# A hybrid decoder step on one core: the sample group's experts all run beside the second block, the low parts of weights are read back by two blocks, the background is spread anew, and attention's score products alternate row halves

## The chip, the cores and the metric

The kernel runs on one core of a Trainium2 chip. The metric is the device time of one execution in microseconds (us). A profiled execution gives the trace from which all rows below come; its time is shown beside its span.

## What is computed

One decoder layer for a prompt of 1024 tokens and a sample group of 8 sequences with 8 tokens each, width 1024. The two groups share all weights. Shortened:

```python
xn = rmsnorm(x, norm1_g)
xr, gr, q, k, v, ga, gb = split(xn @ w_in)              # 1024 x 5632
h  = rg_lru(causal_conv(xr)) ; lru_out = h * gelu(gr)
attn = window_attend(rmsnorm(q), rmsnorm(k), v, sinks)  # window 128, 16 heads on 4 key heads
merged = sigmoid(ga) * (lru_out @ w_branch_lru) + sigmoid(gb) * (attn @ w_branch_attn)
hres = x + merged @ w_out
xt = rmsnorm(hres, norm2_g)
# retrieval: 8 heads, 2 x 128 keys, the 16 best of each, then the best 16 pairs of each head
idx, g = top_pairs(xt @ w_query, sub_keys)              # 128 experts of 16384 for each token
act = gelu(einsum('cd,ced->ce', xt, expert_u[idx])) * g
y = hres + einsum('ce,ced->cd', act, expert_v[idx])
```

The outputs are y for both groups and the new convolution, recurrence and key/value caches.

## The kernel before

**Blocks.** The 1088 tokens go through the layer in three blocks: 256 prompt tokens with the 64 sample tokens, then 384, then 384 prompt tokens. `trunk` does a block in this order: queries, keys and values and the attention (`attention`), the branch of attention (loop of `w_branch_attn`, 8 column chunks), the recurrence (`lru`), the branch of the recurrence (8 chunks), the output product with `w_out` (4 column groups), the second norm (`norm_T`), and the retrieval (`retrieve`). The first norm of the next block (`norm1(bi + 1)`) stands just ahead of `w_out`, and two of the next block's projections (`EARLY`) ahead of the retrieval. After the three blocks, `dense` runs all 16384 experts for 640 prompt tokens, and beside it the last block's 384 tokens fetch their experts row by row.

**Products in two parts.** Each weight chunk of 128 x 1024 numbers is split in a high part (a cast on ScalarE, ACT) and a low part (a subtraction on VectorE, DVE, `split`, L164), and each product is three matmuls (L183 to L185). `wsplit` keeps the low parts of the first block's 84 chunks in HBM (`lo_d`); the third block reads them back (L209) instead of subtracting. High and low parts have three buffers each (`NW = 3`).

**Background.** What a block's retrieval leaves is done beside the next block by a generator, `behind(b)`: first `choose` (17 steps for each token tile: the best pairs of each head), then `build_g`, which turns the prompt tokens' chosen experts into a dense table of gates for `dense` (8 steps of four tokens make a chunk of 32 tokens: 64 steps for block 0, 96 for block 1). A step of `build_g` is two compares on DVE (L940, L941), four scalings on ACT (L943), four products on TensorE (PE, L923; the trace shows each as two instructions) into a PSUM buffer, and a copy by ACT into `sg` (L924). `bg(k)` takes k steps; `PG1` and `PG2` say how many at each place of the second and third block: index 0 after each chunk of the attention branch, 1 after each of six turns of the recurrence, 2 after each chunk of its branch, 3 after each column group of `w_out`, 4 after each tile of the second norm, 5 after each of 16 groups of the retrieval, 6 after each of five parts of q, k and v, 7 after each of 12 score groups. What is left runs at the block's end.

**The sample group's experts** are background too, since their 64 tokens were chosen in block 0. Two rows of partitions share a token, so 64 gathers of 128 rows (512 KB each, issued by GpSimd, POOL, L963) bring the rows of `expert_u`, and DVE multiplies and sums each (`early_u`, L965); 64 more bring `expert_v` (`early_v`, L978, L983). Each uses three row buffers in turn. In the kernel before, `early_u` runs beside the second block and `early_v` beside the third.

**One tile that three things share.** `at` (one buffer) holds a block's keys and values during attention, then the row buffers of `early_u` or `early_v` (tile `et`), then `sg` of `build_g`. PSUM tiles of the tag `tr` (three buffers) serve the transposes of the norms (L268), the products of `build_g` (L923) and the scores of the retrieval (L767). Tiles of one tag are handed out in the order of the program.

**Order.** Each engine carries out its instructions in a fixed order that a scheduler makes ahead of time; SyncE (SP) issues the loads in such an order as well.

Of the kernel before, what the change touches and what calls it, by code (L numbers as in the profile page):

```python
# [14 lines left out]
ALU = mybir.AluOpType  # L15
# [4 lines left out]
P = 128  # L20
# [8 lines left out]
HD = 64  # L29
# [9 lines left out]
SLOPES = [float(np.float32(2.0) ** np.float32(-8.0 * (h + 1) / NH)) for h in range(NH)]  # L39
# [19 lines left out]
NR = 3  # L59
GBL = 1  # L60
PG0 = (0, 0, 0, 0, 0, 0, 0, 0)
PG1 = (5, 5, 4, 5, 2, 2, 0, 0)
PG2 = (6, 6, 5, 1, 2, 4, 2, 2)
LATE = 3
VJ = 1
EARLY = (4, 0)
# [4 lines left out]
def f32(ap):  # L71
    return ap.bitcast(F32)


class Kern:
# [125 lines left out]
    def wsplit(self, key, hi, lo, raw):  # L201

        nc = self.nc
        m = self.chunk.setdefault(key, len(self.chunk))
        use = self.uses[key] = self.uses.get(key, 0) + 1
        kept = self.lo_d[m].rearrange("p (k c) -> p k c", c=raw.shape[2])
        if use == 3:
            nc.scalar.copy(hi, raw)
            nc.sync.dma_start(f32(lo), kept)  # L209
            return  # L210
        self.split(hi, lo, raw)
        if use == 1:
            nc.gpsimd.dma_start(kept, f32(lo))

    def load_c(self, src, c0):

# [79 lines left out]
    def trunk(self, bi, x, raw, bg):  # L296
# [4 lines left out]
        xh, xl = x  # L301
        self.pg = (PG0, PG1, PG2)[bi]
        self.at_free = False
# [98 lines left out]
    def attention(self, bi, xh, xl, ah, al, raw, bg):  # L402
        tc, nc, i, o, sp = self.tc, self.nc, self.i, self.o, self.sp
# [9 lines left out]
        kT = at[:, 2304:2304 + NKV * KC].rearrange("p (k c) -> p k c", k=NKV)  # L413
# [35 lines left out]
        def scores(t, j, qT):  # L449

            c0 = t * P
            first = bi == 0 and t == 0
            b0 = P if first else 0
            S = 2 * P - b0
            sb = sp.tile([P, 4, 256], F32, tag="sb", name="sb", bufs=6)
            for par in range(2):

                pss = self.mm().rearrange("p (g s) -> p g s", s=256)
                pr = slice(par * HD, par * HD + HD)
                for g2 in range(2):  # L460
                    nc.tensor.matmul(pss[:, g2, 0:S], qT[pr, 2 * j + g2, :], kT[pr, j, c0 + b0:c0 + 2 * P], start=True, stop=True)
                for g2 in range(2):
                    g = 2 * g2 + par
                    nc.vector.scalar_tensor_tensor(sb[:, g, 0:S], self.distP[:, b0:], -SLOPES[4 * j + g],
                                                   pss[:, g2, 0:S], op0=ALU.mult, op1=ALU.add)
            sm = sp.tile([P, 4, 4], F32, tag="sm", name="sm", bufs=3)
            m4, z4, e4, nm = (sm[:, x, :] for x in range(4))
            sk = self.snk[:, 4 * j:4 * j + 4]
            nc.vector.tensor_reduce(m4, sb[:, :, 0:S], axis=AX.X, op=ALU.max)
            nc.vector.tensor_tensor(m4, m4, sk, op=ALU.max)  # L470
            nc.vector.tensor_scalar(nm, m4, -1.0, None, op0=ALU.mult)
            nc.vector.tensor_tensor(e4, sk, m4, op=ALU.subtract)
            for g in range(4):
                nc.scalar.activation(sb[:, g, 0:S], sb[:, g, 0:S], AF.Exp, bias=nm[:, g:g + 1], accum_out=z4[:, g:g + 1])
            nc.scalar.activation(e4, e4, AF.Exp)
            nc.vector.tensor_tensor(z4, z4, e4, op=ALU.add)
            nc.vector.reciprocal(z4, z4)
            nc.vector.tensor_tensor(sb[:, :, 0:S], sb[:, :, 0:S], z4.unsqueeze(2).to_broadcast([P, 4, S]), op=ALU.mult)
            return sb
# [28 lines left out]
        for t in range(NT):  # L508
            qT = sp.tile([P, KD, P], F32, tag="sb", name="qT", bufs=6)
            for h in range(2):  # L510
                pt = self.tr()
                for k in range(4):
                    c = (h * 4 + k) * P
                    nc.tensor.transpose(pt[:, k, :], qn[:, t, c:c + P], self.ident)
                nc.scalar.activation(qT[:, 4 * h:4 * h + 4, :], pt, AF.Copy, scale=self.qg[:, 0:1])
            for j in range(NKV):
                late.append((t, j, scores(t, j, qT)))
                bg(self.pg[7])
                if t == 0 and j == (1 if smp else VJ):
                    self.qkv(bi, 5, xh, xl, lambda t, r: vd[0:r, t])  # L520
                if len(late) > (1 if smp else LATE) and (t or j >= VJ):
                    weigh(*late.pop(0))
# [469 lines left out]

    def behind(self, b):

        early, left = None, True
        ch = self.choose(b)
        while left or early is not False:
            if early is None and self.es is not None and self.at_free:
                early = self.early_v() if b else self.early_u()
            if left:  # L1000
                left = next(ch, None) is not None
            if early and next(early, None) is None:
                early = False
            yield True
        for _ in self.build_g(b):
            yield True
# [203 lines left out]
```

## Time and profile before

| what | value |
|---|---|
| median of 3 runs | 3771.19 us (3761.95 to 3776.55) |
| the profiled execution | 3777.02 us, span of its instructions 3775.2 us |
| PE busy / DVE / ACT / POOL | 90% / 77% / 39% / 41% of the span |
| moved by DMA | 968.36 MB, mean 257 GB/s |
| TensorE clock granted, mean | 0.945 of full speed |

The profiled execution is 5.8 us above the median of the runs. In the page, "busy" is the time in which an engine carries out at least one instruction; matmuls are pipelined, so that two of 0.34 us each can start 0.17 us apart. The stretch from the second block to the start of `dense` lies between 489 and 1820 us, `dense` between 1820 and 3775 us.

### The profile page before, as it was taken

The numbers are of one execution on the slowest core, as the hardware profiler recorded it, in microseconds if no ns is written. First come the engines' busy times: TensorE is split into PE (matmuls) and PEld (weight loads), VectorE is DVE, ScalarE is ACT, GpSimd is POOL, SyncE is SP. The second block draws the span as 40 slices with busy tenths as digits, with TensorE's granted clock in tenths as the row PEclk, the third lists the DMA queues.
The fourth block names the chain that finished last, engine by engine and source line by source line (L and its number), as shares of the span: only waits on it lengthen the run. The fifth ranks groups of instructions, "written<-read, shape, count | busy, mean of one in ns | idle before, by whom it ended". The sixth has DMA issues, their size and how long they took to land. (4 is left out here: it accounts for less than half of the span.)

```text
span 3775.2 us, 59354 instructions
## 1 busy us (share of the span) xinstructions
PE 3401.7 (90%) x21891; PEld 3244.8 (86%) x21891; DVE 2889.4 (77%) x6727; ACT 1453.8 (39%) x2969; POOL 1539.4 (41%) x1240
## 2 busy tenths in 40 slices
PE   6898999868898998769779999999999999999996
PEld 6798978758795887668679999999999999999995
DVE  6567797998689975546999777777777776778777
ACT  4555345445854473676222222222222222222220
POOL 0011100340000222000367676767667776777774
PEclk8899999879998999889789999999999999999998
DMA  7388833776552899645478898989989899899897
GB/s 229 108 260 283 264 97 96 242 231 220 183 187 69 272 320 344 238 159 199 162 259 285 314 311 289 312 298 321 311 298 319 307 316 312 310 320 318 310 310 276
DMA packets 539235, 968.36 MB, mean 257 GB/s; under 512 B 38108, under 2 KB 356508, under 8 KB 535840
## 3 DMA queue, kind: packets, MB, share of 16 engines
q0 software_dynamic: 141120, 513.86, 38.1%
q1 hardware_dynamic: 397824, 450.70, 37.5%
q8 instruction: 172, 2.82, 0.3%
q14 instruction: 119, 0.97, 0.1%
HBM read 860.10 MB, written 105.99 MB: 256 GB/s over the span
## 5 line engine op out<-in xcount | busy, mean ns | idle before, releaser
L183 PE MATMUL ou<-ah,vh 128*128 128x256 f32 (+1 forms) x2048 | 637.0, 315 | 58.7 <-DVE dac L1078 30.5
L183 PE MATMUL sc<-dx,uh 128*128 128x256 f32 (+1 forms) x2048 | 636.6, 311 | 11.0 <-DMA gt<-g_d 8.7
L185 PE MATMUL sc<-dx,ul 128*128 128x256 f32 (+1 forms) x2048 | 635.4, 311 | 1.3 <-POOL ul L164 1.3
L184 PE MATMUL sc<-dx,uh 128*128 128x256 f32 (+1 forms) x2048 | 636.2, 311 | 0.0
L184 PE MATMUL ou<-al,vh 128*128 128x256 f32 (+1 forms) x2048 | 632.0, 311 | 3.5 <-DVE al L164 3.2
L185 PE MATMUL ou<-ah,vl 128*128 128x256 f32 (+1 forms) x2048 | 630.3, 310 | 2.5 <-POOL vl L164 2.5
L903 DVE SCALAR_TENSOR_TENSOR acc<-row,hv,acc 128x1024 f32<-128x1024 f32 x384 | 493.6, 1285 | 147.7 <-DMA row<-in_expert_v,iA 145.5
L891 DVE SCALAR_TENSOR_TENSOR row<-row,xt 128x1024 f32<-128x1024 f32 x384 | 464.9, 1216 | 133.6 <-DMA row<-in_expert_u,iA 126.3
L889 POOL DMA_INDIRECT row<-in_expert_u,iA x384 | 366.4, 954 | 279.5 <-DVE row L891 193.2
L901 POOL DMA_INDIRECT row<-in_expert_v,iA x384 | 360.8, 940 | 273.3 <-DVE acc L903 189.9
L183 PEld LDWEIGHTS ou<-ah,vh 128*128 128x128 f32 x2048 | 387.5, 190 | 77.9 <-DVE dac L1078 40.3
L164 POOL TENSOR_TENSOR ul<-un,uh 128x1024 fp32r<-128x1024 f32 x128 | 308.0, 2406 | 330.2 <-DMA gt<-g_d 303.4
L183 PEld LDWEIGHTS sc<-dx,uh 128*128 128x128 f32 x2048 | 392.0, 191 | 12.2 <-ACT uh L163 9.0
L184 PEld LDWEIGHTS ou<-al,vh 128*128 128x128 f32 x2048 | 389.3, 190 | 6.0 <-DVE al L164 5.4
L185 PEld LDWEIGHTS sc<-dx,ul 128*128 128x128 f32 x2048 | 390.9, 191 | 2.1 <-POOL ul L164 2.1
L184 PEld LDWEIGHTS sc<-dx,uh 128*128 128x128 f32 x2048 | 391.9, 191 | 0.0
L185 PEld LDWEIGHTS ou<-ah,vl 128*128 128x128 f32 x2048 | 388.4, 190 | 2.7 <-POOL vl L164 2.7
L1078 DVE TENSOR_TENSOR dac<-dac,ou 128x384 f32<-128x384 f32 (+1 forms) x672 | 314.9, 482 | 46.0 <-PE ou L185 44.9
L163 ACT CAST uh<-un 128x1024 fp32r<-128x1024 f32 x128 | 134.5, 1051 | 496.3 <-PE sc L184 366.7
L164 POOL TENSOR_TENSOR vl<-vn,vh 128x1024 fp32r<-128x1024 f32 x128 | 308.9, 2419 | 16.0 <-ACT vh L163 14.3
L978 POOL DMA_INDIRECT et<-in_expert_v,est x64 | 71.6, 1119 | 585.0 <-DVE oi L940 389.6
L183 PE MATMUL mm<-xh,whi 128*128 128x384 f32 (+1 forms) x768 | 260.1, 339 | 20.1 <-ACT Ti L687 16.8
(294 smaller groups left out, 7655.8 us busy)
## 6 DMA issues: line engine op xcount, KB each, us to landing
wraw<-in_w_in SPq DMA_DIRECT2D x132, 512.0 KB
un<-in_expert_uT SPq DMA_DIRECT2D x128, 512.0 KB
vn<-in_expert_v SPq DMA_DIRECT2D x128, 512.0 KB
lo_d<-wlo POOLq DMA_DIRECT2D x84, 512.0 KB, 5.9
wlo<-lo_d SPq DMA_DIRECT2D x84, 512.0 KB
g_d<-sg SPq DMA_DIRECT2D x20, 2048.0 KB
wraw<-in_peer_w_query SPq DMA_DIRECT2D x48, 512.0 KB
gt<-g_d SPq DMA_DIRECT2D x32, 768.0 KB
```

Source lines behind the costliest of these rows:

```text
L163: nc.scalar.copy(hi, src)
L164: return (lo_eng or nc.vector).tensor_tensor(lo, src, f32(hi), op=ALU.subtract)
L183: nc.tensor.matmul(ps, lh, rh, start=first and j == 0, stop=False)
L184: nc.tensor.matmul(ps, lh, rl, start=False, stop=False)
L185: nc.tensor.matmul(ps, ll, rh, start=False, stop=last and j == n - 1)
L889: nc.gpsimd.indirect_dma_start(out=row, out_offset=None, in_=i["expert_u"], in_offset=bass.IndirectOffsetOnAxis(ap=ia[:, s:s + 1], axis=0))
L891: nc.vector.scalar_tensor_tensor(row, row, 1.0, xt, op0=ALU.mult, op1=ALU.mult, accum_out=hv[:, s:s + 1])
L901: nc.gpsimd.indirect_dma_start(out=row, out_offset=None, in_=i["expert_v"], in_offset=bass.IndirectOffsetOnAxis(ap=ia[:, s:s + 1], axis=0))
L903: nc.vector.scalar_tensor_tensor(acc, row, hv[:, s:s + 1], acc, op0=ALU.mult, op1=ALU.add)
L978: nc.gpsimd.indirect_dma_start(out=row(s), out_offset=None, in_=self.i["expert_v"], in_offset=bass.IndirectOffsetOnAxis(ap=self.es[:, 0, s ...
L1078: nc.vector.tensor_tensor(ac[k // 4][:, k % 4, a:b], ac[k // 4][:, k % 4, a:b], ps[:, 0:b - a], op=ALU.add)
```

## The change

Four things change. `behind` runs `early_u` and then `early_v` beside the second block, two steps of them with each step of `choose` until both are done, and none beside the third. `wsplit` reads the low parts back in the second block too. The tables `PG1` and `PG2` have new numbers; `PG2` takes 22 steps in the third block's attention (34 before). In `scores`, the four products of a group are written one after the other with the upper and the lower row half in turn, into two PSUM tiles taken at once.

```diff
-PG1 = (5, 5, 4, 5, 2, 2, 0, 0)
-PG2 = (6, 6, 5, 1, 2, 4, 2, 2)
+PG1 = (6, 5, 4, 5, 2, 2, 0, 0)
+PG2 = (5, 5, 4, 3, 2, 2, 2, 1)
@@ wsplit
-        if use == 3:
+        if use > 1:
             nc.scalar.copy(hi, raw)
             nc.sync.dma_start(f32(lo), kept)
             return
         self.split(hi, lo, raw)
-        if use == 1:
-            nc.gpsimd.dma_start(kept, f32(lo))
+        nc.gpsimd.dma_start(kept, f32(lo))
@@ attention, scores
-            for par in range(2):
-
-                pss = self.mm().rearrange("p (g s) -> p g s", s=256)
-                pr = slice(par * HD, par * HD + HD)
-                for g2 in range(2):
-                    nc.tensor.matmul(pss[:, g2, 0:S], qT[pr, 2 * j + g2, :], kT[pr, j, c0 + b0:c0 + 2 * P], start=True, stop=True)
...
+            pss = [self.mm().rearrange("p (g s) -> p g s", s=256) for _ in range(2)]
+            for g in range(4):
+                pr = slice(g % 2 * HD, g % 2 * HD + HD)
+                nc.tensor.matmul(pss[g % 2][:, g // 2, 0:S], qT[pr, 2 * j + g // 2, :], kT[pr, j, c0 + b0:c0 + 2 * P], start=True, stop=True)
...
@@ behind
-        early, left = None, True
+        early, left = False if b else None, True
         ch = self.choose(b)
         while left or early is not False:
             if early is None and self.es is not None and self.at_free:
-                early = self.early_v() if b else self.early_u()
+                early = itertools.chain(self.early_u(), self.early_v())
             if left:
                 left = next(ch, None) is not None
-            if early and next(early, None) is None:
-                early = False
+            for _ in range(2):
+                if early and next(early, None) is None:
+                    early = False
             yield True
```

The fixed order of the changed kernel, in two places. Its line numbers after L212 are one lower than before, after L455 three lower (L920 is L923 of before, L267 is L268, L962 is L965, L980 is L983).

The first place is the end of `w_out` in the second block. On DVE, changed kernel (`hr` takes the output product, `et` are the rows of the sample group's experts, `eh` their weights, `oij` and `oi` the compares of `build_g`):

```order
L356 TENSOR_TENSOR hr<-hr,mm 128x256
L962 SCALAR_TENSOR_TENSOR et,eh<-et 128x1024
L356 TENSOR_TENSOR hr<-hr,mm 128x256 x2
L962 SCALAR_TENSOR_TENSOR et,eh<-et 128x1024 x4
L965 TENSOR_TENSOR eh<-eh,est 128x64
L978 TENSOR_SCALAR et<-et,eh 128x1024
L980 SCALAR_TENSOR_TENSOR et<-et,eh 128x1024 x63
L985 TENSOR_TENSOR et<-et 64x1024
L986 TENSOR_TENSOR et<-et 64x1024
L938 TENSOR_TENSOR oij<-iof,sT 128x512 x2
```

Behind the last `hr` stand the last four rows of `early_u` and all 64 of `early_v`, with nothing between them, and then `build_g`. On PE, the same place before (`gh`, `gl` are the operands of `w_out`, `xn` the rows that a norm transposes):

```order
L185 MATMUL mm<-whi,gl 128x256
L923 MATMUL tr<-oij 128x128 x64
L268 MATMUL tr<-ident,xn 128x128 x4
L183 MATMUL mm<-whi,xh 128x256
L184 MATMUL mm<-wlo,xh 128x256
```

and in the changed kernel:

```order
L185 MATMUL mm<-whi,gl 128x256
L920 MATMUL tr<-oij 128x128 x92
L267 MATMUL tr<-ident,xn 128x128 x4
L183 MATMUL mm<-whi,xh 128x256
L184 MATMUL mm<-wlo,xh 128x256
```

16 steps of `build_g` (64 products) stood between `w_out` and the next norm's transposes, now 23 do (92), and none of these that needs `sg` can be copied out before `early_v` has left `at`.

The second place is the end of `w_out` in the third block, on PE, before:

```order
L185 MATMUL mm<-whi,gl 128x256
L923 MATMUL tr<-oij 128x128 x56
L737 MATMUL tr<-ident,st 4x128 x8
L923 MATMUL tr<-oij 128x128 x176
L268 MATMUL tr<-ident,xn 128x128 x8
L923 MATMUL tr<-oij 128x128 x8
```

and in the changed kernel:

```order
L185 MATMUL mm<-whi,gl 128x256
L920 MATMUL tr<-oij 128x128 x12
L267 MATMUL tr<-ident,xn 128x128 x8
L920 MATMUL tr<-oij 128x128 x8
L267 MATMUL tr<-ident,xn 128x128 x8
```

58 steps of `build_g` stood behind the third block's `w_out`, now 3 do. Between the third block's attention and the end of its `w_out` PE has products of 79 steps in the changed kernel, one or a few at a time among the matmuls, and of 3 before; in the retrieval behind it some 9 are left, before some 35.

## Rows read from the trace of the kernel before

**Rows 1.** Busy time of the second block's attention; columns stand in rows 2.

```profile
489.00:604.00 115.00, 101.09 (x611) 77.81 (x610) 102.35 (x368) 68.09 (x192) 0.00 (x0) 0.93 0.16 48
```

**Rows 2.** Busy time by stretch, in us from the span's start; columns in the first line.

```profile
core 0: us, PE busy (x) PEld busy (x) DVE busy (x) ACT busy (x) POOL busy (x), PEclk, DMA share, GB/s
...
604.00:923.00 319.00, 269.93 (x1481) 252.44 (x1479) 290.17 (x692) 137.03 (x213) 79.61 (x64) 0.90 0.69 218
923.00:951.00 28.00, 18.21 (x132) 16.53 (x130) 16.45 (x33) 26.61 (x79) 0.00 (x0) 0.88 0.47 168
951.00:1149.00 198.00, 177.10 (x1256) 173.52 (x1256) 152.35 (x606) 131.87 (x320) 0.00 (x0) 0.95 0.59 197
1149.00:1246.00 97.00, 82.37 (x365) 55.66 (x366) 96.00 (x368) 55.34 (x169) 0.00 (x0) 0.82 0.14 43
1246.00:1543.00 297.00, 261.80 (x1490) 246.67 (x1488) 205.32 (x380) 130.44 (x206) 71.60 (x64) 0.96 0.96 321
1543.00:1677.00 134.00, 82.59 (x531) 76.73 (x531) 76.14 (x172) 116.18 (x335) 0.00 (x0) 0.80 0.46 172
1677.00:1820.00 143.00, 122.29 (x727) 114.28 (x725) 95.42 (x438) 69.35 (x171) 0.00 (x0) 0.86 0.49 170
1820.00:3740.00 1920.00, 1846.55 (x12303) 1822.99 (x12304) 1510.42 (x2657) 475.49 (x789) 1334.72 (x1015) 0.98 0.88 303
```

**Rows 3.** Groups on DVE, 604 to 923 us: count, busy us, mean ns, idle before.

```profile
L965 DVE SCALAR_TENSOR_TENSOR et<-et 128x1024 f32<-128x1024 f32 x64 | 77.8, 1218 | 8.3 <-DMA et<-in_expert_u,est 8.2
L164 DVE TENSOR_TENSOR wlo<-wraw,whi 128x1024 fp32r<-128x1024 f32 x52 | 63.1, 1214 | 3.0 <-ACT whi L163 3.0
L823 DVE TENSOR_TENSOR eq<-ce,bf 128x800 f32<-128x800 f32 (+1 forms) x24 | 23.6, 982 | 0.1
```

**Rows 4.** Gathers of L963 (second block), then of L978 (third block).

```profile
DMA to landing us min/median/max: 4.2/5.2/8.7
...
DMA to landing us min/median/max: 4.2/7.1/11.2
```

**Rows 5.** Timelines near 850 us: a row is used, and the next gather starts.

```profile
849.89 1.23 DVE L965 SCALAR_TENSOR_TENSOR et<-et 128x1024 f32<-128x1024 f32 x1 [0.85 <-DMA et<-in_expert_u,est]
...
851.40 0.94 POOL L963 DMA_INDIRECT et<-in_expert_u,est  x1 [2.31 <-DVE et L965]
```

**Rows 6.** Timelines of DVE and PE where `early_v` ends and `build_g` starts.

```profile
1524.86 2.60 DVE L983 SCALAR_TENSOR_TENSOR et<-et,eh 128x1024 f32<-128x1024 f32 x2
...
1537.60 1.22 DVE L988 TENSOR_TENSOR et<-et 64x1024 f32<-64x1024 f32 x1 [4.17 <-DMA et<-et]
...
1545.76 2.62 PE L923 MATMUL tr<-oij 128*128 128x128 f32 x22
```

**Rows 7.** Groups of all engines, 1543 to 1677 us.

```profile
L943 ACT ACTIVATE oij<-oi,sT 128x128 f32<-128x128 bf16 x248 | 79.4, 402 | 3.1 <-DVE oi L940 2.3 <-PE tr L923 0.6
L923 PE MATMUL tr<-oij 128*128 128x128 f32 x496 | 78.0, 324 | 49.2 <-ACT sg L924 46.4 <-ACT so L738 1.7 <-DVE yl L164 0.8
...
L941 DVE TENSOR_TENSOR oij<-iof,sT 128x512 f32<-128x512 f32 x62 | 42.0, 689 | 35.0 <-PE tr L923 34.4
L924 ACT COPY sg<-tr 128x512 f32<-128x512 f32 x64 | 35.3, 582 | 18.1 <-PE tr L923 7.0 <-DMA g_d<-sg 6.8 <-DMA out_y<-et 4.3
```

**Rows 8.** What PE waited for, 1246 to 1543 us: us, times, longest.

```profile
PE mm L183 <- DVE hr L357: 11.9, 1, 11.9
PE mm L185 <- DMA wlo<-lo_d: 5.3, 6, 2.6
```

**Rows 9.** Timeline of PE: neighbours of 384 columns, and of 256.

```profile
1460.86 0.34 PE L183 MATMUL mm<-lh,whi 128*128 128x384 f32 x1
1461.03 0.34 PE L184 MATMUL mm<-ll,whi 128*128 128x384 f32 x1
...
919.01 0.28 PE L183 MATMUL mm<-whi,gh 128*128 128x256 f32 x1
919.13 0.28 PE L184 MATMUL mm<-wlo,gh 128*128 128x256 f32 x1
```

More of the change, by code (lines that the diff above doesn't have):

```diff
@@ L455, in scores @@
             sb = sp.tile([P, 4, 256], F32, tag="sb", name="sb", bufs=6)
-            for par in range(2):
-                pss = self.mm().rearrange("p (g s) -> p g s", s=256)
-                pr = slice(par * HD, par * HD + HD)
-                for g2 in range(2):
-                    nc.tensor.matmul(pss[:, g2, 0:S], qT[pr, 2 * j + g2, :], kT[pr, j, c0 + b0:c0 + 2 * P], start=True, stop=True)
[L462 to L465, printed above, removed]
+            pss = [self.mm().rearrange("p (g s) -> p g s", s=256) for _ in range(2)]
+            for g in range(4):
+                pr = slice(g % 2 * HD, g % 2 * HD + HD)
+                nc.tensor.matmul(pss[g % 2][:, g // 2, 0:S], qT[pr, 2 * j + g // 2, :], kT[pr, j, c0 + b0:c0 + 2 * P], start=True, stop=True)
+            for g in range(4):
+                nc.vector.scalar_tensor_tensor(sb[:, g, 0:S], self.distP[:, b0:], -SLOPES[4 * j + g],
+                                               pss[g % 2][:, g // 2, 0:S], op0=ALU.mult, op1=ALU.add)
             sm = sp.tile([P, 4, 4], F32, tag="sm", name="sm", bufs=3)
```

## The prediction

> **What bounds the kernel now.** I read the page first, then the busy time by stretch [rows 1, 2], since the change lies in the second and the third block alone. `dense` (1820 to 3740 us) has PE busy 1847 of 1920 us at a DMA share of 0.88 [rows 2]; the change gives it the same work, so I let it stand and look at the 1331 us from 489 to 1820. There the bound changes from stretch to stretch, and the reader should see four different ones. From 604 to 923 (second block, from its attention branch to the end of `w_out`) DVE is busy 290 of 319 us: it carries the rows of `early_u` and the subtractions of low parts beside the block's own work [rows 2, 3]. The same stretch of the third block, 1246 to 1543, has DVE at 205 of 297 us and DMA at 0.96: no subtractions, but low parts from HBM and the rows of `early_v` [rows 2]. At 1149 to 1246, the third block's attention, DVE is busy 96 of 97 us. And from 1543 to 1677 nothing is full: PE has 83 of 134 us, DVE 76, ACT 116 [rows 2]. This is `build_g` run on its own, in a chain in which PE waits 46 us for ACT's copies and DVE 34 us for PE [rows 7]; the second norm and the retrieval stand behind it. It begins there because `sg` shares its buffer with `early_v`, which ends at 1527.5; the first products follow at 1545.8 [rows 6].
>
> **The change part by part.** All terms are changes against the profiled execution.
>
> *Second block, 604 to 923.* 52 subtractions of 1.214 us leave DVE, 63 us [rows 3]; their place is taken by 52 reads of 512 KB. By the order `early_u` ends four rows later than this stretch, so 60 of its 64 rows stay. What is left is nearly what the third block does in 1246 to 1543 now: no subtractions, low parts from HBM, one set of gathers. That took 297 us, against 319: **-22 us**. PE's own need (below) is some 255 us at its clock there, so the bounds are -45 (all but some ten of its waits gone) and 0 (the loads cost what the subtractions did).
>
> *The end of the second block's `w_out`.* Here the order matters most. DVE has 68 rows in a row, four of `early_u` and 64 of `early_v`. PE has 92 products ahead of the next transposes of a norm; three fit into the `tr` buffers, the rest need `sg`, and that waits for `early_v`. So PE has nothing to do while the rows come in. Three row buffers are in use. Where DVE did not queue, a row was used from 849.89 to 851.12, and the next gather started at 851.40, 0.28 us later [rows 5]. A cycle is then the landing, 0.28 us and DVE's 1.3 (2.60 for two) [rows 6]. With the second block's median landing of 5.2 us it is 6.78 us for three rows, 2.26 a row; with the minimum of 4.2, 1.93; with the third block's 7.1, where DMA was full, 2.89 [rows 4]. I take 2.25, since the low and high parts fetched ahead are soon stopped by three buffers, while three gathers still share the engines. 68 x 2.25 = 153 us. To this come some 5 us for the first landing, the end of `early_v` (18 us from the last row to the first product of `build_g`, of which 10 wait for a copy between partitions on a full DMA [rows 6]; I take 14), and 23 steps of `build_g`. A step costs ACT four scalings of 0.32 and a copy of 0.55, 1.83 us [rows 7]; 23 are 42, and since some compares and scalings are made ahead, 40. Sum 212 us, in place of the 28 us that 16 steps take there now [rows 2]: **+184 us**. Bounds from the cycle alone: +162 and +228. Nothing covers this: the retrieval, the next block's projections and everything behind them stand after those transposes on PE.
>
> The Trainium skill ("DMA: Bandwidth & Descriptors", section on the anatomy of a DMA from GpSimd) fits such a transfer as 2.0 us plus the bytes at 436 GB/s, which gives an estimate of 3.2 us for 512 KB. The trace's least landing is 4.2 and its median 5.2 us [rows 4], so I go by the rows. By the page's figure a row would take (3.2 + 0.28 + 1.3) / 3 = 1.59 us, and the sum would be 68 x 0.66 = 45 us lower.
>
> *The rest of the second block, 951 to 1149.* 16 subtractions of the retrieval's weights go (19 us of DVE), and eight steps of `build_g` have been done ahead (15 us of ACT). DVE is at 152 of 198 us, ACT at 132, PE at 177 [rows 2], so not all of it shows: **-20 us**, between 0 and -34. Of the second block's subtractions ten, 12 us, stand before 604, where DVE is busy 102 of 115 us beside PE's 101 [rows 1]: **-5 us**, between 0 and -12.
>
> *Third block's attention.* `PG2` takes 22 steps of `choose` here instead of 34. DVE is full; a step is a top-16 of some 1 us or a pair like L823's of 2 x 0.98 [rows 3], so 12 steps are some 17 us of DVE. **-12 us**, as ACT and PE have chains there too; bounds -17 and 0. The scores' new order changes the order of PE's work in the two attentions, and PE isn't what lasts there (82 of 97 us); holding two of three `mm` buffers at once may cost as much. Nothing.
>
> *Third block, 1246 to 1543.* 64 rows leave (80 us of DVE, 34 MB of DMA), and 76 more steps of `build_g` come in. PE's need now: 48 chunks of 24 matmuls of 384 columns, 0.174 us apart (three in 0.52), 200 us; 288 of 256 columns, 0.118 apart, 34 [rows 9]; the gates some 10; sum 245, and 255 at the granted 0.96. PE waited 12 us for `hr`, which DMA brought late, 5 for low parts [rows 8], and the rest in the recurrence. 76 steps of 8 instructions, 0.12 us apart (22 in 2.62 [rows 6]), add 72: 317 us, 323 at a clock of 0.98. ACT goes from 130 to 130 + 76 x 1.83 = 269, DVE from 205 to some 210, DMA to some 82 MB of the 95 now moved. PE is now the bound. With half of today's waits (19 us) kept, 342: **+45 us**; bounds +20 (all waits filled, full clock) and +70 (all kept, and more where PE waits in order for ACT).
>
> *The 134 us behind it* shrink to the norms with eight steps among them: 8 x 1.83 is 15, and the norms need about as long again, 30: **-104 us**, between -112 and -95. *The retrieval, 1677 to 1820:* 26 steps fewer, 26 x 8 x 0.12 = 25 us of PE, 26 x 1.83 = 48 of ACT and with two compares each (0.69 and 0.42) 29 of DVE, whose queue ended last there: PE is busy 122 of 143 and DVE 95 [rows 2]. I take 100 us: **-43**, between -25 and -50.
>
> **Sum.** Second block -22 + 184 - 20 - 5 = +137. Third block -12 + 45 - 104 - 43 = -114. Together +23 us: 3777 + 23 = 3800 against the profiled execution. This is 5.8 us above the median, so I forecast 3771 + 23 = **3794 us**.
>
> **The rivals.**
>
> *Faster: rows come at DVE's pace.* If the landings of three gathers overlap well enough, DVE's 1.3 us sets the pace: 68 x 1.3 = 88 instead of 153, a net of -42, 3729 us. For it: the stretch has nearly no other DMA. Against it: three buffers and a landing of 4.2 us at least [rows 4]. It decides when a row takes less than 1.63 us (23 + 19 = 42 us over 68 rows). The skill's fit, above, would put it just there. With what small errors of the other terms in the same direction would do, chance 0.22.
>
> *Even.* The third block hides its steps better (+20 instead of +45) and the rest goes as forecast: net -2, 3769. For it: PE had 35 us of waits in 1246 to 1543, part of them for a DMA that gets 34 MB less [rows 2, 8]. Against it: PE and ACT must fall into step, in a fixed order. Chance 0.29.
>
> *Worse: the rows land as in the third block,* 2.89 us each: +44 more, net +67, 3838. For it: that is the only place in the rows where three `early_v` buffers ran [rows 4]. Against it: DMA was at 0.96 there. Chance 0.14. The forecast keeps 0.35.
>
> **How the numbers follow.** A change under 0.5% (19 us) could hardly be told from none with this kernel. Forecast and worse case are slower by more, 0.49; even 0.29; faster 0.22. The forecast's own range is 3780 to 3820. The range for 8 in 10 reaches from 3738, close to the first rival, to 3846, just past the third.
>
> **What would show it.** In the changed profile: a stretch of some 200 us behind the second block's `w_out` with PE nearly idle, DVE busy a little over half with one line, POOL at the same pace, and PE's waits there on ACT's copy to `sg`, which waits for `early_v`'s output. Gathers in it 2.0 to 2.5 us apart. No stretch of PE on `build_g` alone in the third block; its norms 30 us behind `w_out`. 1246 to 1543's counterpart some 340 us long with PE over 90% busy. I am wrong if the rows run at under 1.63 us, or if `early_v` is found spread under the matmuls of the second block, or if the third block's long stretch stays near 297 us or goes past 370.

## The result and the profile after

The changed kernel takes 3790.31 us (median of 20 runs, 3778.95 to 3807.41) against 3774.5 us for the kernel before on the same chip: a ratio of 1.0051, 95% interval 1.0039 to 1.0064. So the change costs about half a per cent; 3794 us were forecast. Its profiled execution took 3790.05 us, a span of 3788.3, 13.1 us more than before.

Busy time by stretch, changed kernel. The columns are those of [rows 2], and the stretches end at the same events; the retrieval ends with the first product of `dense`, which before was at 1825 us, where [rows 2] has its border at 1820.

```profile
593.00:890.00 297.00, 262.76 (x1488) 249.73 (x1487) 230.39 (x633) 138.60 (x223) 64.92 (x62) 0.96 0.94 312
890.00:1105.00 215.00, 29.15 (x189) 27.51 (x188) 113.47 (x122) 39.51 (x111) 65.61 (x66) 0.56 0.64 206
1105.00:1281.00 176.00, 159.08 (x1128) 155.58 (x1127) 124.69 (x562) 112.91 (x269) 0.00 (x0) 0.97 0.70 236
1281.00:1380.00 99.00, 85.30 (x430) 61.12 (x429) 95.58 (x369) 61.00 (x178) 0.00 (x0) 0.86 0.23 72
1380.00:1724.00 344.00, 327.42 (x2105) 317.10 (x2104) 209.56 (x497) 265.19 (x614) 0.00 (x0) 0.98 0.74 241
1724.00:1748.00 24.00, 14.21 (x91) 13.05 (x90) 13.74 (x40) 14.75 (x37) 0.00 (x0) 0.72 0.97 363
1748.00:1849.00 101.00, 88.23 (x552) 86.69 (x552) 79.75 (x437) 34.02 (x66) 0.00 (x0) 0.95 0.56 186
1849.00:3788.00 1939.00, 1849.56 (x12328) 1827.34 (x12328) 1518.06 (x2638) 474.56 (x790) 1342.60 (x1024) 0.98 0.88 304
```

The second row is the one to see: 215 us behind the second block's `w_out` in which PE is busy 29, where the kernel before had 28 us in all. The third block is the counterpart: 344 us with PE at 327 instead of 297 at 262, and behind it 24 and 101 us instead of 134 and some 148. `dense` starts 24 us later than before (1849 for 1825) and is 11 us shorter.

What PE waited for from 890 to 1105 us (total, times, longest):

```profile
PE tr L920 <- ACT sg L921: 185.2, 6, 171.8
```

The longest of these waits ends where `early_v` does. Timeline of all engines there:

```profile
1051.66 1.28 DVE L980 SCALAR_TENSOR_TENSOR et<-et,eh 128x1024 f32<-128x1024 f32 x1 [1.61 <-DMA et<-in_expert_v,est]
1052.98 0.52 SPq L983 DMA_DIRECT2D et<-et  x1
1055.93 1.22 DVE L985 TENSOR_TENSOR et<-et 64x1024 f32<-64x1024 f32 x1 [2.98 <-DMA et<-et]
...
1058.42 0.49 SPq L987 DMA_DIRECT2D out_y<-et  x1
1061.45 1.56 ACT L921 COPY sg<-tr 128x512 f32<-128x512 f32 x3 [157.13 <-DMA out_y<-et]
...
1062.09 4.21 PE L920 MATMUL tr<-oij 128*128 128x128 f32 x18 [171.80 <-ACT sg L921]
```

In order stand the last row, the copy between partitions, the two additions and the output; only when that has left the shared tile come ACT's first copies into `sg`, and behind them PE. The answers to [rows 4] follow: the landing (from a gather's issue until its data has arrived) of the gathers of `early_u` (beside the matmuls), then of `early_v`:

```profile
DMA to landing us min/median/max: 4.3/7.2/11.8
...
DMA to landing us min/median/max: 4.2/5.1/6.1
```

DVE's groups from 593 to 890 us and from 890 to 1105; the 52 subtractions of [rows 3] are gone:

```profile
L962 DVE SCALAR_TENSOR_TENSOR et<-et 128x1024 f32<-128x1024 f32 x59 | 71.7, 1217 | 16.1 <-DMA et<-in_expert_u,est 16.1
...
L980 DVE SCALAR_TENSOR_TENSOR et<-et,eh 128x1024 f32<-128x1024 f32 x63 | 80.9, 1284 | 62.4 <-DMA et<-in_expert_v,est 62.2
```

### The profile page after: what moved, and what is told of

Its sections match the earlier page's. It is cut to its first block, busy times and chain, and to the rows that moved or that the text cites. A ratio compares the mean times of both kernels' runs of the same rounds, so it can differ in the third digit from the quotient of the medians.

```text
span 3788.3 us, 59373 instructions
## 1 busy us (share of the span) xinstructions
PE 3345.3 (88%) x21891; PEld 3216.4 (85%) x21891; DVE 2796.3 (74%) x6643; ACT 1451.0 (38%) x2971; POOL 1518.2 (40%) x1240
## 4 chain that ended last, share of the span: by engine, by line
PE 24%; DMA 19%; DVE 11%; issue 8%; POOL 7%; ACT 5%; SPq 0%; POOLq 0%; DVEq 0%; ACTq 0%
DMA row<-in_expert_u,iA 6%; DMA row<-in_expert_v,iA 6%; DMA et<-in_expert_v,est 3%; POOL row L886 3%; PE ou L183 3%; PE ou L184 3%; PE ou L185 2%; PE mm L185 2%; DVE row L888 2%; PE mm L184 2%; PE mm L183 2%; PE tr L920 2%; PE sc L183 2%; PE sc L184 2%; PE sc L185 2%
## 5 line engine op out<-in xcount | busy, mean ns | idle before, releaser
L183 PE MATMUL ou<-ah,vh 128*128 128x384 f32 (+1 forms) x2048 | 634.8, 315 | 50.8 <-ACT ah L163 22.1
L184 PE MATMUL ou<-al,vh 128*128 128x384 f32 (+1 forms) x2048 | 632.7, 311 | 2.1 <-DVE al L164 2.0
L185 PE MATMUL ou<-ah,vl 128*128 128x384 f32 (+1 forms) x2048 | 630.9, 311 | 0.6 <-POOL vl L164 0.6
L920 PE MATMUL tr<-oij 128*128 128x128 f32 x1280 | 177.5, 291 | 209.2 <-ACT sg L921 205.5
L920 PEld LDWEIGHTS tr<-oij 128*128 128x128 f32 x1280 | 170.2, 206 | 216.1 <-ACT sg L921 209.1
```

The source lines that it names most:

```text
L183: nc.tensor.matmul(ps, lh, rh, start=first and j == 0, stop=False)
L184: nc.tensor.matmul(ps, lh, rl, start=False, stop=False)
L185: nc.tensor.matmul(ps, ll, rh, start=False, stop=last and j == n - 1)
L920: nc.tensor.matmul(pt[:, x, :], oj[:, x], wi[:, x], start=True, stop=True)
```

## The experiments

Twelve kernels in four groups; each group ran on one chip with the kernel before, and ratios are to that. "The transposes" are the second block's first transposes of a norm behind `w_out`. Each kernel left one profile, so a difference of a few us between two stretches may be that of two executions.

### The parts one by one

**Low parts alone.**

```diff
-        if use == 3:
+        if use > 1:
...
-        if use == 1:
-            nc.gpsimd.dma_start(kept, f32(lo))
+        nc.gpsimd.dma_start(kept, f32(lo))
```

> The kernel before, with only the second block's low parts read back instead of subtracted. Theory A (the terms of the prediction: subtractions that leave DVE are gains of their own, the rows of the experts are a loss of their own): the second block's stretch up to the end of w_out is 15 to 25 us shorter, what stands ahead of it 5 to 10, the retrieval behind it 10 to 20; nothing else moves: 3725 to 3745 us, 30 to 50 us below the kernel before. Theory B (the reads cost DMA what the subtractions cost DVE, and the 22 us seen in the changed kernel came from rows and steps that moved out of the stretch): 3762 to 3785 us.

Measured: 3755.57 us, ratio 0.9956 (0.9940 to 0.9971), between the two theories. `w_out` ended at 884 us, 40 us earlier than before, but the gain shrank at once. DVE and PE at the end of `w_out`, and the gathers of `early_u`:

```profile
903.13 1.22 DVE L964 SCALAR_TENSOR_TENSOR et<-et 128x1024 f32<-128x1024 f32 x1 [1.25 <-DMA et<-in_expert_u,est]
...
905.18 10.33 PE L922 MATMUL tr<-oij 128*128 128x128 f32 x64 [21.41 <-ACT sg L923]
...
DMA to landing us min/median/max: 4.3/7.5/10.4
```

The rows of `early_u` now land in 7.5 us instead of 5.2 [rows 4]; the last is used at 903 us, 19 us behind `w_out`, and until then PE waits 21 us at products that need `sg`. So the transposes stood 46 us behind `w_out` instead of 28, and the lead had shrunk to 21 us. In the third block `early_v` has the same length as before and `w_out` ends 29 us earlier, so 19 us more (153 instead of 134) are spent behind it. It follows that reads and rows are not two terms: the reads that took work from DVE here made the rows late.

**The order of the score products alone** (the diff of `scores` above). 

> The kernel before, with only the new order of the score products. The third block's attention took 99 us in the changed kernel and 97 before, although it had 12 steps of choose fewer. Theory A (the order is worth nothing, the steps that left it weren't what set its length): attention 97 us, time within 8 us of before. Theory B (taking two PSUM tiles at once costs what the 12 steps gave back): attention 105 to 112 us, and the time 8 to 25 us above before. Theory C (alternating row halves overlap on TensorE): attention 85 to 92 us and 8 to 25 us below before.

Measured: 3778.23 us, ratio 1.0023 (1.0007 to 1.0038). The attention of the third block took 99 us, 97 before; the profiled span was even 0.4 us shorter than before. This is theory A, with a small loss (7 us by the medians); the alternating halves gain nothing.

**The experts and the tables alone.**

```diff
-PG1 = (5, 5, 4, 5, 2, 2, 0, 0)
-PG2 = (6, 6, 5, 1, 2, 4, 2, 2)
+PG1 = (6, 5, 4, 5, 2, 2, 0, 0)
+PG2 = (5, 5, 4, 3, 2, 2, 2, 1)
...
-                early = self.early_v() if b else self.early_u()
+                early = itertools.chain(self.early_u(), self.early_v())
```

> The kernel before, with only the experts' rows all beside the second block and the new tables; the subtractions and the old order of the scores stay. Theory A (the row-by-row wait behind w_out is a loss of this part alone): some 215 us between the end of w_out and the norm's transposes, the third block 105 to 115 us shorter as in the changed kernel, and without the gains of the low parts 3825 to 3855 us, 50 to 80 us slower than before. Theory B (the reads of low parts make the rows late): rows come at under 1.7 us each, the wait is 160 us or less, and the time 3790 us or less.

Measured: 3794.19 us, ratio 1.0064 (1.0045 to 1.0083), below theory A. The third block behaved as in the changed kernel (345, 23 and 101 us). The second differs, by stretch:

```profile
602.00:922.00 320.00, 269.89 (x1460) 251.20 (x1458) 295.35 (x692) 136.87 (x211) 102.51 (x82) 0.89 0.75 237
922.00:1093.00 171.00, 33.75 (x212) 32.64 (x213) 100.72 (x115) 42.45 (x122) 50.99 (x46) 0.58 0.61 199
```

82 gathers, not 62, were issued by the end of `w_out`, since without reads `early_u` was through at 867 us, and the wait behind is 171 us instead of 215. So the row-by-row wait is a loss of this part alone (A's mechanism), but 44 us of its 215 come from the reads (B's). They do not come at B's pace, under 1.7 us a row: gathers of `early_v` were still issued every 2.4 us (median), but 48 rows stood behind `w_out` instead of 69. Both theories priced the parts wrongly: the 22 us that the reads save in the stretch and the 44 that they add behind it belong together. The ratios of the three parts add up to +0.43%, the whole was +0.51%; each has an interval of 0.1 to 0.2% either way.

### What holds the block up behind w_out

**The table changed.**

```diff
-PG1 = (6, 5, 4, 5, 2, 2, 0, 0)
+PG1 = (6, 5, 0, 1, 0, 4, 0, 0)
```

> The changed kernel with another table for the second block: no step of build_g is placed between the attention branch and the norms behind w_out, four instead of two with each tile of norms' projections, and what is left runs at the block's end. Theory A (the wait behind w_out is there because the norms' transposes stand behind products that need sg, thus early_v, in the fixed order): the norms' transposes start within 40 us of the end of w_out, and part of the retrieval runs beside the rows; some 40 to 50 steps of 2 us run alone at the block's end instead. 3710 to 3765 us. Theory B (the rows themselves hold the block up, through DVE's queue or the shared tile, whatever stands ahead on TensorE): 3780 to 3800 us.

Measured: 3803.68 us, ratio 1.0074 (1.0047 to 1.0101). The transposes started 8 us behind `w_out`, as A said, but PE's waits from 888 to 1256 us were:

```profile
PE tr L920 <- ACT sg L921: 131.1, 4, 129.4
```

It is the same wait, now inside the retrieval, where steps of `build_g` stand between its groups. The second block ended 25 us earlier, the third block's attention took 20 us more, and `dense` started at 1849 us as in the changed kernel. A's mechanism is shown for where PE waits; its gain was not there.

**Own PSUM buffers.**

```diff
-            pt = self.tr()
+            pt = self.pp.tile([P, 4, P], F32, tag="po", name="pg", bufs=2)
```

> The changed kernel with two PSUM buffers of their own for the products of build_g, which thus no longer share the buffers of the norms' transposes and of the retrieval's scores; the tables stay. Theory A (TensorE stands still behind w_out because products that need sg hold, in the fixed order, both TensorE's queue and the shared PSUM buffers): the norms' transposes start within 30 us of the end of w_out, but the retrieval still stands behind build steps through the buffers of its loads; the second block ends 20 to 50 us earlier, 3740 to 3770 us. Theory B (the placement by the table alone matters, not the shared buffers): the wait of 198 us on the copy to sg stays, 3780 to 3800 us.

The tag `po` adds no PSUM buffer: its two buffers are those of the attention's output, which nothing else in a block uses. "Own buffers" below means these.

Measured: 3773.53 us, ratio 1.0021 (1.0002 to 1.0040), 3.5 us above A's range. The transposes started 6 us behind `w_out`; PE then waited 174 us for `sg`, 129.7 of them in one piece before 1095 us, and the retrieval ended at 1288 us, no earlier than in the changed kernel. The profiled span was 6 us shorter, by 13 us in the third block, so for the second block A's gain is a miss: the wait has moved into the retrieval, where PE's next instruction is again a product of `build_g`. The loads of the retrieval's keys share their SBUF buffers with `build_g` too, as the expectation says; no run tested that apart.

**Both together.** 

> Both together: no step of build_g between the attention branch and the norms of the second block, and PSUM buffers of its own for its products. The table alone started the norms 9 us behind w_out, but TensorE then stood 129 us at the first product that needs sg, in the retrieval. Theory A: now norms, projections and the retrieval run beside the 128 rows, some 55 steps of build_g follow alone at the end (110 us), and the second block ends at 1160 to 1200 us in place of 1281: 3680 to 3720 us. Theory B (DVE, which has the rows, the retrieval's compares and the norms, makes rows or retrieval late by as much): the block ends at 1240 us or later, 3755 to 3790 us.

Measured: 3767.38 us, ratio 0.9992 (0.9979 to 1.0006). Three stretches of 30 us, the one from 1040 us with no PE at all:

```profile
980.00:1010.00 30.00, 30.00 (x219) 30.00 (x218) 29.28 (x134) 8.82 (x13) 6.56 (x7) 1.00 0.97 342
...
1040.00:1070.00 30.00, 0.00 (x0) 0.00 (x0) 28.00 (x29) 0.00 (x0) 14.93 (x13) 0.50 0.69 209
...
1130.00:1160.00 30.00, 16.97 (x104) 15.44 (x104) 12.50 (x24) 20.63 (x60) 0.00 (x0) 0.75 0.22 80
```

The norms and the whole retrieval ran beside the rows and were done at 1016 us, 265 us earlier than in the changed kernel. But the last gather was issued at 1118 us and the last row used at 1125, 72 us later than in the changed kernel. Then 62 steps of `build_g` had to follow alone up to 1270, and only then could the next attention have the shared tile: it ended at 1367 us instead of 1380. A's first half is right, but B's figures came true, and at least in part for B's reason. While the retrieval ran, DVE was busy 29 of 30 us and 7 gathers were issued; afterwards it was 13 (POOL's count in the first two rows). DMA was at 0.97 in the first row too, so how much of the delay is DVE's stays open. What is late next is the tile `at`.

**Two row buffers.**

```diff
-            row = et[:, D * (1 + s % 3):D * (2 + s % 3)]
+            row = et[:, D * (1 + s % 2):D * (2 + s % 2)]
```

(the same in `early_v`). 

> The changed kernel with two row buffers in place of three, nothing else. Theory A (behind w_out a row's pace is a whole cycle, from the gather's issue over its landing to DVE's last read and the next issue, divided by the number of buffers): the 2.31 us between gathers there become 3.2 to 3.5, the wait behind w_out grows by 60 to 80 us, and early_u ends later still: 3850 to 3900 us. Theory B (GpSimd's issue or a fixed rate of the indirect transfers sets the pace): 2.3 to 2.5 us a row as before, time within 15 us of the changed kernel. A pace between 2.5 and 3.2 would say that a gather lands sooner when fewer share the engines.

Measured: 3857.47 us, ratio 1.0236 (1.0211 to 1.0261); the wait behind `w_out` grew from 215 to 295 us. Timeline of gathers and rows with two buffers:

```profile
999.90 0.94 POOL L975 DMA_INDIRECT et<-in_expert_v,est  x1 [1.64 <-DVE et L980]
1001.51 1.28 DVE L980 SCALAR_TENSOR_TENSOR et<-et,eh 128x1024 f32<-128x1024 f32 x1 [1.88 <-DMA et<-in_expert_v,est]
1003.07 0.94 POOL L975 DMA_INDIRECT et<-in_expert_v,est  x1 [2.23 <-DVE et L980]
1004.19 1.28 DVE L980 SCALAR_TENSOR_TENSOR et<-et,eh 128x1024 f32<-128x1024 f32 x1 [1.39 <-DMA et<-in_expert_v,est]
```

A gather issued at 999.90 is used at 1004.19, 4.3 us later; with 1.28 us of DVE and 0.28 to the next issue the cycle is 5.9 us, and the measured median pace 2.88. With three buffers the pace was 2.31, a cycle of 6.9 us. So the cycle through the buffers sets the pace (A), but not at A's 3.2 to 3.5 us: from issue to use the median was 4.2 us with two buffers and 5.2 with three, so a gather lands about one us sooner when two share the engines, as the expectation's last sentence allowed. That the wait still grew by A's 80 us has a second cause, more rows behind `w_out`: 17 of `early_u`, not 5.

```profile
L962 DVE SCALAR_TENSOR_TENSOR et<-et 128x1024 f32<-128x1024 f32 x17 | 20.8, 1225 | 32.0 <-DMA et<-in_expert_u,est 32.0
```

### Where the tile is taken next

**The first block's build_g done in the third block** (on top of the previous kernel of both edits).

```diff
-PG1 = (6, 5, 0, 1, 0, 4, 0, 0)
-PG2 = (5, 5, 4, 3, 2, 2, 2, 1)
+PG1 = (6, 5, 0, 0, 0, 0, 0, 0)
+PG2 = (8, 7, 5, 4, 2, 2, 2, 2)
...
-        for _ in self.build_g(b):
-            yield True
+        for d in (0, 1) if b == 1 else () if b == 0 else (b,):
+            for _ in self.build_g(d):
+                yield True
```

> The previous kernel (own PSUM buffers, nothing ahead of the norms), with the first block's 64 steps of build_g left out of the second block and done in the third, ahead of the second block's 96. Theory A (a step of build_g costs some 2.2 us alone and 0.6 to 1 us among the third block's products; the 128 rows end at 1118 us whatever is done with it): the third block's attention branch starts at 1215 to 1245 us in place of 1367, its stretch to the end of w_out grows from 340 to 390 to 420 us, retrieval up to 15 us longer: 3670 to 3715 us. Theory B (ScalarE's five instructions a step become the bound in the third block): that stretch takes 450 us or more, 3740 us or more.

Measured: 3781.19 us, ratio 1.0011 (0.9995 to 1.0027). The attention branch started at 1230 us and the stretch to the end of `w_out` took 399, both as A said. The miss is behind them. PE's groups from 1629 to 1817 us:

```profile
L920 PE MATMUL pg<-oij 128*128 128x128 f32 x400 | 54.0, 283 | 4.3 <-ACT sg L921 4.3
```

50 steps were still left there, and norms and retrieval took 188 us instead of 120. `dense` took 1968 us, 24 more than in the kernel it was made from; no cause for that is known.

**The same, subtracting in the second block** (`use == 3` again). 

> The same, but the second block subtracts its low parts again, as the kernel before does. Theory A (the reads of low parts make each row beside the second block take 3.4 to 3.7 us instead of 2.8, and rows are what the third block's attention waits for): w_out ends 25 to 35 us later, the rows end 40 to 70 us earlier, at 1050 to 1080 us, and the attention with them; 20 to 60 us below the run with reads: 3640 to 3680 us. Theory B (DVE's subtractions cost the second block what the rows gain): within 10 us of the run with reads.

Measured: 3757.26 us, ratio 0.9950 (0.9930 to 0.9971). The last gather was issued 70 us earlier, at 1048 us, as A said, but the attention branch started only 12 us earlier (1218): the retrieval, which was done at 1015 us with reads, now ended at 1123. So for the blocks B is nearer: of the 40 us between the two profiled spans 12 stand at the attention branch and 27 in `dense`, which was back at 1941 us. By the medians the two kernels are 24 us apart.

### Reads and buffers, four cells and a mixture

**Low parts read, and own PSUM buffers** (both edits from above on the kernel before). 

> The kernel before with the second block's low parts read back, and with PSUM buffers of its own for build_g. With the reads alone w_out ended 38 us earlier, but the norms' transposes stood 46 us behind it instead of 30, since the rows of early_u ended at the same time as w_out and build_g's products hold the PSUM buffers. Theory A (that is where the gain went): the transposes start 5 to 15 us behind w_out, the second block ends 20 to 40 us earlier than with the reads alone or the retrieval waits instead; 3725 to 3750 us. Theory B (steps of build_g only move to the block's end, where they run alone): 3750 to 3770 us.

Measured: 3734.32 us, ratio 0.9890 (0.9867 to 0.9912), as A said: transposes 6 us behind `w_out`, second block's end 34 us earlier than with reads alone, and in the third block 62 us instead of 153 between `w_out` and the retrieval's projections, of which the retrieval gave 66 back (215 instead of 149).

**Own PSUM buffers alone.** 

> The kernel before with PSUM buffers of its own for build_g, and nothing else; it is the fourth of the cells without and with reads of low parts, without and with own buffers. Theory A (own buffers free the norms behind w_out wherever build_g stands, and this was worth 17 to 90 us beside the reads): the transposes start within 10 us of the end of w_out in both blocks, the third block's stretch of build_g on its own shrinks by 50 us or more but the retrieval takes most of it up: 3735 to 3755 us, and the reads are worth 10 to 30 us beside own buffers. Theory B (own buffers help only where the reads have made room on DVE): within 8 us of the kernel before.

Measured: 3720.81 us, ratio 0.9880 (0.9852 to 0.9908): better than A, and A's last clause is a miss, since beside own buffers the reads are worth nothing (0.9890 with them). The profile has the second block up to the end of `w_out` and behind it, and the third block up to `w_out`, behind it, and the retrieval:

```profile
610.00:954.00 344.00, 292.54 (x1687) 274.82 (x1685) 313.59 (x743) 180.79 (x344) 80.46 (x64) 0.91 0.68 216
954.00:1100.00 146.00, 145.62 (x1070) 144.91 (x1068) 132.25 (x551) 105.72 (x251) 0.00 (x0) 1.00 0.69 228
1209.00:1507.00 298.00, 262.55 (x1497) 247.35 (x1496) 199.06 (x354) 129.61 (x202) 72.36 (x64) 0.97 0.96 320
1507.00:1570.00 63.00, 33.06 (x203) 29.82 (x201) 35.35 (x94) 45.34 (x127) 0.00 (x0) 0.73 0.47 172
1570.00:1780.00 210.00, 165.98 (x1056) 157.58 (x1056) 137.76 (x561) 143.43 (x385) 0.00 (x0) 0.89 0.51 180
```

The transposes start as `w_out` ends, and PE never stops from 954 to 1100 us; before, these parts took 28 and 198 us [rows 2]. `w_out` itself ended 31 us later, since with the edit the fixed order holds 26 steps of `build_g` ahead of that point instead of 2: the buffers act through the order too. The second block ended 49 us earlier; the lead is 37 us where the third block's attention branch starts and 46 us at the end. The third block's stretch keeps its 298 us, with DMA at 0.96, and behind it 63 us stand in place of 134, which the retrieval gives back (210 instead of 148), as A said; there the transposes stood 50 us behind `w_out`, not 10.

**Reads with a third of the chunks subtracted** (on the kernel with reads and own buffers).

```diff
-        if use > 1:
+        if use > 1 and m % 3:
...
-        nc.gpsimd.dma_start(kept, f32(lo))
+        if use == 1:
+            nc.gpsimd.dma_start(kept, f32(lo))
```

> The run with reads and own buffers, with a third of the chunks subtracted instead of read in the second and third blocks. Theory A (reads make the experts' rows late, and rows set when build_g starts): the rows of early_v take 3.2 to 3.6 us instead of 3.78, end 15 to 35 us sooner, build_g with them, and the kernel is 10 to 25 us below the run with reads alone: 3710 to 3725 us. Theory B (DVE's 1.21 us a subtraction cost as much): 3730 to 3750 us.

Measured: 3688.43 us, ratio 0.9791 (0.9767 to 0.9815), 32 us below own buffers alone in the same group, below A's range, and the fastest of all. The rows of the third block came every 3.07 us (median) and the last was issued at 1446 instead of 1483 us (A's mechanism), with DMA at 0.90 instead of 0.95:

```profile
1205.00:1500.00 295.00, 267.53 (x1555) 254.28 (x1553) 229.22 (x397) 141.37 (x238) 78.65 (x64) 0.97 0.90 297
1500.00:1535.00 35.00, 22.96 (x140) 20.64 (x139) 23.14 (x73) 32.34 (x90) 0.00 (x0) 0.76 0.71 245
```

What was 62 us behind `w_out` with all low parts read is 35; 86 steps of `build_g` were left there instead of 94. Against own buffers alone, 4 us of the gain stand at the end of the second block and 35 at the start of `dense`. So most of it comes from the third block, where both earlier kernels read all low parts. A kernel that subtracts a third there alone, or all, was not run.

## Why the prediction was right, step by step

Forecast and trace, both against the profiled execution before, in us:

| stretch | forecast | measured |
|---|---|---|
| ahead of the second block's attention branch | -5 | -11 |
| attention branch to end of `w_out` | -22 | -22 (319 to 297) |
| end of `w_out` to the norm's transposes | +184 | +187 (28 to 215) |
| rest of the second block | -20 | -22 (198 to 176) |
| third block's attention | -12 | +2 (97 to 99) |
| third block to end of `w_out` | +45 | +47 (297 to 344) |
| norms behind it | -104 | -110 (134 to 24) |
| retrieval | -43 | -47 |
| `dense` and the end | 0 | -11 |
| sum | +23 | +13 |

Up to `dense` the terms sum to +24 where +23 were forecast, and that closeness is luck in part: 14 us too many at the third block's attention are made up by 18 us in four other terms (6 ahead of the branch, 6 at the norms, 4 at the retrieval, 2 in the rest of the second block). The medians put the change at 16 us; 3794 lies so near to 3790 also because the kernel before ran 3 us slower beside the changed one than in the three runs that the forecast starts from.

**The wait behind `w_out`** came out by its own working. The landing was taken as the second block's median of 5.2 us and was 5.1, the pace 2.25 and was 2.31 a row, and the last row to the first of the waiting products took 10.4 us of the 14 allowed. That PE's order and the shared buffers put this wait ahead of the transposes is shown by the runs with another table and with own buffers, in which the transposes start 5 to 8 us behind `w_out` while the rows still come in. That the rows set its length, by holding the tile, is shown by the same runs: PE stands 129 and 130 us in one piece there too, at a later place. The rival "rows at DVE's pace" fell: DVE waited 62 us for landings there.

The Trainium skill ("DMA: Bandwidth & Descriptors", section on the anatomy of a DMA from GpSimd) gives an estimate of 3.2 us for such a transfer; the trace doesn't agree, since the least landing here was 4.2 us, and with two in flight a row was used 4.2 us after its issue (median). By that estimate the stretch would have been 45 us shorter.

**The third block** hid 76 steps at +47 us: PE is busy 327 of 344 us, so PE's own time is the price, as worked out. The "even" rival, with +20, fell.

**The one step outside its stated bounds is the third block's attention,** -12 forecast and +2 measured. The working read 12 steps fewer from the table `PG2`. DVE's groups there, before and changed:

```profile
L823 DVE TENSOR_TENSOR eq<-ce,bf 128x800 f32<-128x800 f32 x8 | 7.9, 982 | 0.0
...
L813 DVE MAX8 bv<-c 128x8 f32<-128x50 f32 x13 | 2.7, 204 | 0.1
```

```profile
L820 DVE TENSOR_TENSOR eq<-ce,bf 128x800 f32<-128x800 f32 x8 | 7.8, 978 | 0.0
...
L810 DVE MAX8 bv<-c 128x8 f32<-128x50 f32 x13 | 2.7, 205 | 0.0
```

Eight pairs and 13 second halves of a top-16 in both: nearly the same work stands there. The table says behind what a step is written, not where it stands in DVE's fixed order; the working took PE's places from the order and these from the table. The same stretch with the new score order alone, and with experts and tables alone, shows that neither moved it by more than some 2 us from its 97:

```profile
1146.00:1245.00 99.00, 81.90 (x369) 55.21 (x370) 97.53 (x378) 55.78 (x170) 0.00 (x0) 0.81 0.14 42
...
1274.00:1370.00 96.00, 76.83 (x367) 53.03 (x368) 93.72 (x354) 56.83 (x171) 0.00 (x0) 0.88 0.17 54
```

**Two reasons were right for the whole and wrong for the parts.** The terms -22 and +184 were added as if independent. They are not: alone, the experts' part waits 171 us, and the reads alone lose 18 us again behind `w_out`, because the landing goes from 5.2 to over 7 us beside reads. The sum held since the row count behind `w_out` (68) was read from the order with both in.

**`dense`,** forecast at 0, came out 11 us shorter. Over the kernels here it took 1939 to 1968 us, though none of the edits is in it: 1940 with the new score order alone, 1954 with experts and tables alone. The executions of the kernel before alone spread over 26 us in one group (3754.9 to 3780.8), so one profile of each kernel cannot tell a cause from chance here. The 11 us are put down to no part of the change; what sets them stays open.

## What to carry to other kernels

Work put into the background should share no resource that the foreground takes in program order: here a shared set of PSUM buffers cost more (1.2%) than the whole change moved, and beside the changed kernel each cure of the order or the buffers only moved the wait to the next place that needed the shared tile. A load that relieves one engine can make the transfers beside it late, so it need not be all or nothing: a third subtracted and the rest read, beside own buffers, gave the fastest kernel, 2.1% below the kernel before. Whether that beats subtracting everything is not shown. And a table of steps is not an order: count what stands on the engine.

## What the hardware showed

A gather of 128 rows of 4 KB landed in 5.1 us at the median with three in flight and little else, in 7.1 to 7.6 us beside reads of low parts (DMA at 0.94 to 0.97), and was used 4.2 us after its issue (median) with two in flight; a third buffer therefore bought 20% of pace (2.88 to 2.31 us), not a third.
